# A two-layer attention trunk: compressed values and gate spread in row tiles, a sixth weight buffer, and a list schedule with pauses and an order table

## The chip, the cores and the metric

The kernel runs on one core of one Trainium2 chip. The core has a matrix engine (TensorE, PE in the profile; its weight loads are PEld), a vector engine (VectorE, DVE), a scalar engine (ScalarE, ACT), GpSimd (POOL) and a queue engine (SyncE, SP) that issues most loads. The metric is the device time of one execution in microseconds. All arithmetic is done in fp32 or in pairs of its rounded halves.

## The reference

`x` is 256 tokens of 1024 features. Each of two layers does `x = x + gate * mixer(h)`, where `shift, scale, gate` come from the vector `c` through `ada_w[i]` (1024 x 3072), and `h` is the RMS norm of `x`, scaled and shifted. Both mixers project `h`, attend with 16 query heads over 4 key heads of 64 features, multiply by `silu(z)` and project out:

```python
shift, scale, gate = split(silu(c) @ ada_w[i] + ada_b[i], 3)
h = rms_norm(x, norm_g[i]) * (1 + scale) + shift
# layer 1 (nsa): three attentions, each with its own gate per head
o = g0 * o_cmp + g1 * o_slc + g2 * o_win
# layer 2 (moba): with 256 tokens one block, so plain causal attention
x = x + gate * ((o * silu(z)) @ w_out)
```

In layer 1 `o_cmp` attends over 15 compressed keys and values: blocks of 32 tokens go through a small two-layer network per key head (`cmp_w1`, `cmp_w2`). `o_slc` and `o_win` come out, at this length, as two causal attentions with different keys and values.

## The kernel before

**Products.** An fp32 matrix is split into a rounded part `hi` and a rest `lo` (lines 624 to 631: ACT casts, DVE subtracts), and a product is three matmuls: hi by hi, hi by lo, lo by hi. A weight piece of 256 rows by 512 columns (512 KB) is loaded into one of five buffers `raw` (line 450) by SP; the last reader of `raw` is the subtraction into `lo`. PSUM has eight banks: two go by the name `acc`, for long accumulations, and six by the name `ps`, for everything else (lines 447, 448).

**Stages.** To about 58 us the first rows of `ada_w` and of the input projection are loaded into their own early buffers and multiplied as they land. Then come the rest of layer 1's projection with the compression network on its side, `make_q`, and eight pairs of heads (`pair_a(i)`, lines 1290 to 1331), with blocks of the `z` projection and layer 2's `ada_w` between them. The output projection (`out_products`) ends with the update of `x` and layer 2's norm (`next_h`, line 1348). Layer 2 does the same with `pair_b`, and its output projection ends in the stores.

**The two places in layer 1 that change.** The compressed attention of four pairs at once (`compressed(hf)`, line 1262) leaves `pcT[hf]`: 128 rows, which are 8 heads of 16 compressed keys, by 256 tokens. Pair `j_` needs only rows `32*j_` to `32*j_ + 31`. The kernel before multiplies all 128 rows by a matrix `Vbd[:, hf, j_]` that is zero outside those rows (lines 1239 to 1249 build it with the mask `emask`); the result starts the accumulation of the pair's output `o`, a `ps` bank, which `values` then adds to:

```python
o = tile_of("ps", 512)
T.matmul(o[:, 0:S], Vbd[:, hf, j_], pcT[hf], start=True, stop=False)
```

`values` (line 899) and the products by `condz` (line 640) use column tiles: parts of the matrix engine's columns, chosen by `tile_position`, so that several small products go on beside each other. The other place is `ada_gate(0)` (line 696): the gate of layer 1 arrives as row sums in `g`, and two full fp32 products with the 0/1 matrices `selG` add and spread them over all 128 partitions.

**Order.** Nothing is issued as the program runs. Each call records an operation with its dependencies, its buffers and a cost in ns (`record`, `_cost`), numbered in the order of the program. `Plan.issue` (line 231) then plays a list schedule: it keeps a clock for each engine, a clock for the DMA wire, and the times at which buffers come free; each step it takes, over all engines, the operation that can start first, ties going by level (urgent chain, chain, fill) and then by number. In that order the instructions are issued on each engine, loads into SP's queue included. The clocks of this planner decide only the order; on the chip each engine waits for semaphores. A product in column tiles that follows another one in tiles has a level of its own (`_rank`, line 223), and a change of the tiling adds 240 cycles of cost (line 335). All instructions carry the line of one helper, L373, so that they are told apart by the names of their tiles.

Of the kernel before, what the change touches and what calls it, by code (L numbers as in the profile page):

```python
# [9 lines left out]
F32 = mybir.dt.float32  # L10
# [4 lines left out]
OP = mybir.AluOpType  # L15
AX = mybir.AxisListType

P = 128
S = 256
# [3 lines left out]
HD = 64  # L23
# [11 lines left out]

TICK = 10240 / 3
DEEP = 2e4
TILED, LATER = -0.5, 0
SHORT_ROWS, SMALL, BEHIND, EARLY_RATE = 1.1, 7e4, 5500.0, 348.0
ISSUE, FIRST_BYTE, RATE, LANDED = 450.0, 1500.0, 315.0, 700.0  # L40


class Tag:
# [9 lines left out]
class Plan:  # L53
# [120 lines left out]
    def _cost(self, engine, method, args, kw, aps):  # L174
        def free(a):
            n = 1
            for _, k in a.ap[1:]:
                n *= k
            return n

        if "dma" in method:
            self.bytes = free(aps[0]) * aps[0].shape[0] * 4
            if aps[1].shape[-1] <= 128 and self.bytes > 1e5:
                self.bytes *= SHORT_ROWS
            if self.bytes <= 1e5:
                self.bytes += SMALL
            return max(ISSUE, self.bytes / RATE) if engine == "S" else ISSUE
        psum = any(str(a.space).endswith("PSUM") for a in aps)
        n = max(free(a) for a in aps)
        if engine == "T":  # L190
            if method == "transpose":
                return 262.0 if aps[1].dtype == F32 else 180.0
            cols = free(aps[2])
            if aps[2].dtype == F32:
                m = free(aps[1])
                if "tile_position" in kw and m <= 64:
                    return max(cols * 4.28 * max(32, m) / P, 60.0)
                return 2 * max(cols * 2.14, 264.0)
            return max(cols * (1.07 if aps[2].dtype == F32R else 1.0), 264.0)
        if engine == "A":  # L200
            return 0.833 * n + (51.0 if psum else 94.0) + 93.0 * sum(isinstance(kw.get(k), bass.AP) for k in ("bias", "scale", "accum_out"))
        if engine == "G":
            return 1.5 * n + 270.0
        if method == "reciprocal":
            return 6.5 * n + 68.0
        fast = not psum and (method == "tensor_copy" or method.startswith("tensor_scalar"))
        pointers = len(aps) - 2 if method.startswith("tensor_scalar") else 0
        return (0.521 if fast else 1.042) * n + 68.0 + 61.0 * pointers
# [22 lines left out]
    def issue(self, opening=()):  # L231
# [21 lines left out]
        for waiting, for_, call in opening:  # L253
            left = sum(len(self.tags[f].tiles) for f in for_)
            gate = {"left": left, "for": set(for_), "end": 0.0, "call": call, "called": False}
# [20 lines left out]
        tally, mode = {}, None  # L276
        ready = {e: [] for e in self.engines}
        for op in ops:
            op["at"] = 0.0
            if not op["wait"]:  # L280
                ready[op["engine"]].append(op)
        done = 0
        while done < len(ops):
            best = None
            for e, ops_e in ready.items():
                if not ops_e:
                    continue
                found = []
                first = None
                for op in ops_e:  # L290
                    t = max(clock[e], op["at"])
                    if first is not None and t > first and not (op["level"] < 0 and t <= first + self.AHEAD):
                        continue
                    blocked = False
                    for n in op["needs"]:
                        r = room(n)
                        if r is None:
                            blocked = True
                            break
                        t = max(t, r)  # L300
                    if blocked:
                        continue
                    found.append((t, self._rank(op, e, mode), op["id"], op))
                    first = t if first is None else min(first, t)
                pick = min(found, key=lambda f: f[:3]) if found else None
                if pick:
                    soon = [f for f in found if f[1] < 0 and f[1] < pick[1] and f[0] <= pick[0] + self.AHEAD
                            and f[0] < pick[0] + pick[3]["cost"]]
                    if soon:
                        pick = min(soon, key=lambda f: (f[1], f[0], f[2]))  # L310
                if pick and (best is None or pick[0] < best[0]):
                    best = pick + (e,)
            start, _, _, op, e = best
            ready[e].remove(op)
            for n in op["needs"]:
                t = self.tiles[n]
                if t["slot"] is None:
                    tag = t["tag"]
                    gate = closed.get(tag.name)
# [3 lines left out]
                    slot = min(tag.free)  # L323
# [8 lines left out]
            cost = op["cost"]  # L332
            if e == "T":
                tick = int(start // TICK)
                if op["mode"] != mode:
                    cost += 240.0
                mode = op["mode"]
                cost = cost * (1 / 2.4 if tally.get(tick - 1, 0.0) >= 3060.0 else 1 / 1.2)
                tally[tick] = tally.get(tick, 0.0) + op["cost"]
            end = start + cost  # L340
            clock[e] = end
            seen = end + self.SEEN[e]
# [10 lines left out]
            for n in op["needs"]:  # L353
                t = self.tiles[n]
# [11 lines left out]
            for a in after[op["id"]]:  # L366
                b = ops[a]
# [33 lines left out]
def kernel(  # L401
# [23 lines left out]
    nc = tc.nc  # L425
    ctx.enter_context(tc.manual_schedule())
    const = ctx.enter_context(tc.tile_pool(name="const", bufs=1))
    work = ctx.enter_context(tc.tile_pool(name="work", bufs=1))
    psum = ctx.enter_context(tc.tile_pool(name="psum", bufs=1, space=bass.MemoryType.PSUM))
    plan = Plan(nc)  # L430
    T, A, V, G, Q = plan.T, plan.A, plan.V, plan.G, plan.S
    tile_of = plan.tile
# [14 lines left out]
    plan.tag("acc", psum, 512, 2, space="PSUM")  # L447
    plan.tag("ps", psum, 512, 6, space="PSUM")
    plan.tag("early", early["pool"], 1024, 12)
    plan.tag("raw", work, 1024, 5)  # L450
    plan.tag("hi", work, 1024, 4, F32R)
    plan.tag("lo", work, 1024, 4, F32R)
    plan.tag("n_in", work, 1024, 2)
# [73 lines left out]
    nc.gpsimd.memset(maskC, 0.0)  # L527
    for m in range(2):
        keep(maskC[:, m, :], [[-16, 16]], m * P - 31)
    selG = const.tile([P, 2, P], F32, name="selG")  # L530
    nc.gpsimd.memset(selG, 0.0)
    nc.gpsimd.memset(selG[0:64, 0, :], 1.0)
    nc.gpsimd.memset(selG[64:128, 1, :], 1.0)
    ones = const.tile([P, P], F32, name="ones")
    nc.gpsimd.memset(ones, 1.0)
    identR = const.tile([P, P], F32R, name="identR")
    V.tensor_copy(identR, identF)
    emask = const.tile([P, 8], F32, name="emask")
    V.tensor_reduce(emask, identF.rearrange("p (j n) -> p j n", n=16), axis=AX.X, op=OP.add)


    RT = const.tile([P, ROWS], F32, name="RT")
# [153 lines left out]
    def ada_gate(l):  # L696

        gate = gates_of[l] = tile_of("gate", D)
        bias = bass.AP(tensor=ada_b.tensor, offset=ada_b.offset + l * 3 * D + 2 * D, ap=[[D, 1], [1, D]])
        if l:  # L700
            G.memset(gate, 0.0)
            Q.dma_start(gate[0:1], bias)
            for kk in range(8):
                w = ada_piece(l, kk, 2 * D, D)[:, 0, :]
                with plan.at(FILL):
                    V.scalar_tensor_tensor(gate, w, condz[:, kk, 0:1], gate, op0=OP.mult, op1=OP.add)
                yield
            mix, src = (ones, ones), (gate[:, 0:512], gate[:, 512:1024])
        else:
            g = yield from ada_rows(l, (2 * D, 2 * D + 512), 512)  # L710
            for s in range(2):
                Q.dma_start(g[64 * s + 1:64 * s + 2], bias[:, s * 512:(s + 1) * 512])
            mix, src = (selG[:, 0], selG[:, 1]), (g, g)
        for s in range(2):
            t = tile_of("ps", 512)
            with plan.at(FILL):
                T.matmul(t, mix[s], src[s], start=True, stop=True)
                A.copy(gate[:, s * 512:(s + 1) * 512], t)
# [350 lines left out]
    for k in range(2):  # L1069
# [16 lines left out]
        a, b = lead_w[k]  # L1086
# [149 lines left out]
                        kcs[:, 0, part].rearrange("p a d -> p (a d)"), identR[0:64, 0:64])  # L1236
    A.copy(KTA[:, :, :, 512:528], tk[:, 0:128].rearrange("p (a g n) -> p a g n", a=2, g=KVH))
    vb = tile_of("ps", 512)
    Vbd = const.tile([P, 2, 4, P], F32, name="Vbd")
    for hf in range(2):  # L1240
        for cc in range(2):
            uv = tile_of("pc", 2, 4, 16)
            V.tensor_copy(uv, u[:, cc, 1, 32 * hf:32 * hf + 32].rearrange("p (g n) -> p g n", g=2)[:, :, None, :]
                          .to_broadcast([P, 2, 4, 16]))
            T.matmul(vb[:, hf * HD:(hf + 1) * HD], uv.rearrange("p g r n -> p (g r n)"), w2[:, 1, cc, :],
                     start=(cc == 0), stop=(cc == 1))
        V.tensor_mul(Vbd[:, hf].rearrange("p j (e d) -> p (j e) d", e=2),
                     vb[:, None, hf * HD:(hf + 1) * HD].to_broadcast([P, 8, HD]),
                     emask[:, :, None].to_broadcast([P, 8, HD]))

    raw_q = tile_of("n_in", 2, 512)
    chunk(w_in, ((512, 512),), raw_part(raw_q, 512))
# [4 lines left out]
    z_later = z_blocks(w_in, 3120, zT)  # L1257


    pcT = {}  # L1260

    def compressed(hf):

# [26 lines left out]
    def pair_a(i):  # L1290
# [28 lines left out]
        for r in (1, 0):  # L1319
# [4 lines left out]
                return p1[r][:, e, 0, k * P:(k + 1) * P]  # L1324

            pT.insert(0, p_transposed(block))
        o = tile_of("ps", 512)
        T.matmul(o[:, 0:S], Vbd[:, hf, j_], pcT[hf], start=True, stop=False)
        vs = slice(g * HD, (g + 1) * HD)
        values(o, [([VA[:, m, 1 - r, vs] for m in range(2)], pT[r]) for r in (1, 0)], False)  # L1330
        gated(i, o, zT[i])
# [169 lines left out]
```

## Time and profile before

| | us |
|---|---|
| median of 3 runs | 317.1 (315.71 to 317.89) |
| profiled execution | 317.45 |
| its span | 315.7 |
| PE busy | 306.0 |
| PEld / DVE / ACT / POOL busy | 243.5 / 242.2 / 205.0 / 26.6 |
| DMA | 65.82 MB, mean 208 GB/s |

A row of a group names the line, the engine, the operation, `out<-in` by the names of the tiles, their shapes and the count; then the busy time, the mean length of one in ns, and the idle time in front. An fp32 product shows as two MATMUL instructions, a product of rounded halves as one. Matmuls overlap, so the distance between two starts, not the length, is what one costs. In the chain a row gives start, length and what the time went to.

### The profile page before, as it was taken

What the parts mean: (1) busy time and instruction counts of PE and PEld (TensorE: products, weight loads), DVE (VectorE), ACT (ScalarE), POOL (GpSimd) and SP (SyncE); (2) the same over time, 40 slices, a digit from 0 to 9 for tenths busy, and PEclk for the clock granted to TensorE, in tenths of its full rate; (3) what the DMA queues carried; (4) which work ended last, traced back from release to release, by engine and by line L of the source; (5) the groups of instructions that cost most, each with busy time, mean ns of one, the idle gap of its engine ahead of it and who ended that gap; (6) DMA issues with size and microseconds to landing.
All of it is one profiled execution on the core that took longest, in us unless ns stands there. A gap on an engine that the chain in (4) does not pass through costs nothing.

```text
span 315.7 us, 6158 instructions
## 1 busy us (share of the span) xinstructions
PE 306.0 (97%) x2133; PEld 243.5 (77%) x2133; DVE 242.2 (77%) x734; ACT 205.0 (65%) x486; POOL 26.6 (8%) x102
## 2 busy tenths in 40 slices
PE   4999999998999999999999999999999999999995
PEld 4666677777766797858879888877788999968784
DVE  4673374669982899835979887998599999999764
ACT  5735155764835787456799966786486489998420
POOL 8248900000000000000000000000000000000000
PEclk9999999999999999999999999999999999999999
DMA  7999999359899822788272377617188862423102
GB/s 248 320 357 367 368 359 323 111 171 311 279 309 306 277 79 90 246 304 250 113 261 76 116 217 226 240 60 212 65 261 263 298 229 84 155 69 120 59 34 102
DMA packets 44174, 65.82 MB, mean 208 GB/s; under 512 B 4221, under 2 KB 20971, under 8 KB 44142
## 3 DMA queue, kind: packets, MB, share of 16 engines
q1 hardware_dynamic: 43782, 65.36, 63.1%
q8 instruction: 17, 0.28, 0.4%
q14 instruction: 15, 0.12, 0.1%
q10 hardware_dynamic: 168, 0.06, 0.1%
q0 software_dynamic: 192, 0.00, 0.0%
HBM read 64.36 MB, written 1.05 MB: 207 GB/s over the span
## 4 chain that ended last, share of the span: by engine, by line
PE 90%; DMA 5%; ACT 2%; DVE 1%; issue 1%; SPq 0%; ACTq 0%; DVEq 0%
PE ps L373 54%; PE acc L373 36%; DMA raw<-in_nsa_w_in_dram 2%; DMA early<-in_ada_w_dram 2%; ACT hi L373 1%; DMA rot<-in_c_dram 0%; ACT n_in L373 0%; DVE lo L373 0%; DVE p L373 0%; ACT p L373 0%; DVE AB L373 0%; ACT HT L373 0%; DVE rot L373 0%; DVE y L373 0%; DVE X L373 0%
## 5 line engine op out<-in xcount | busy, mean ns | idle before, releaser
L373 ACT CAST hi<-raw 128x1024 fp32r<-128x1024 f32 (+1 forms) x48 | 48.8, 1023 | 25.5 <-DMA raw<-in_nsa_w_in_dram 9.8
L373 DVE TENSOR_TENSOR lo<-raw,hi 128x1024 fp32r<-128x1024 f32 (+1 forms) x48 | 56.4, 1181 | 11.0 <-ACT hi L373 10.8
L373 PE MATMUL acc<-hi,HT 128*128 128x512 f32 (+1 forms) x160 | 49.6, 381 | 1.3 <-ACT n_in L373 0.8
L373 ACT ACTIVATE p<-p,tiny 128x128 f32<-128x128 f32 (+1 forms) x96 | 43.2, 460 | 8.4 <-DVE tiny L373 8.3
L373 PE MATMUL acc<-HT,hi 128*128 128x256 f32 x192 | 37.8, 286 | 0.0
L373 PEld LDWEIGHTS acc<-hi,HT 128*128 128x128 f32 x160 | 29.1, 188 | 9.6 <-issue 2.9
L373 DVE CUSTOM_DVE_ANT_0 p<-ps,causal 128x128 f32<-128x128 f32 (+1 forms) x96 | 30.5, 346 | 3.1 <-PE ps L373 3.1
L373 PEld LDWEIGHTS acc<-HT,hi 128*128 128x128 f32 x192 | 30.1, 188 | 0.8 <-issue 0.7
L373 PE MATMUL acc<-lo,HT 128*128 128x512 f32 (+1 forms) x80 | 30.2, 380 | 0.2 <-DVE lo L373 0.2
L373 PE MATMUL ps<-hi,HT 128*128 128x512 f32 (+1 forms) x96 | 28.2, 365 | 0.0
L373 PE MATMUL acc<-HT,lo 128*128 128x256 f32 x96 | 27.8, 290 | 0.0
L373 PE MATMUL ps<-KTA,qg 128*128 128x256 f32 (+2 forms) x192 | 27.0, 284 | 0.0
L373 ACT COPY pT<-ps 128x384 f32<-128x384 f32 x48 | 21.5, 485 | 6.3 <-PE ps L373 6.2
L373 PEld LDWEIGHTS ps<-KTA,qg 128*128 128x128 f32 x192 | 24.2, 190 | 1.7 <-issue 1.2
L373 PE MATMUL ps<-hi,qg 128*128 128x256 f32 (+1 forms) x96 | 24.1, 323 | 0.0
L373 PE MATMUL acc<-hi,qg 128*128 128x512 f32 x64 | 22.8, 402 | 0.0
L373 PE MATMUL ps<-identF,p 128*128 128x128 f32 x144 | 21.7, 276 | 0.0
L373 PEld LDWEIGHTS ps<-hi,HT 128*128 128x128 f32 x96 | 17.0, 188 | 4.2 <-issue 2.1
L373 PEld LDWEIGHTS ps<-identF,p 128*128 128x128 f32 x144 | 16.4, 140 | 3.9 <-issue 1.2
L373 ACT ACTIVATION_READ_ACCUMULATOR p<-p,tiny 128x1 f32 x96 | 19.3, 201 | 0.0
L373 PE MATMUL ps<-pT,VA 128*64 128x256 f32 (+1 forms) x192 | 19.1, 334 | 0.0
L373 PEld LDWEIGHTS acc<-HT,lo 128*128 128x128 f32 x96 | 18.1, 189 | 0.1
(223 smaller groups left out, 614.5 us busy)
## 6 DMA issues: line engine op xcount, KB each, us to landing
raw<-in_ada_w_dram SPq DMA_DIRECT2D x32, 512.0 KB, 4.9
raw<-in_moba_w_in_dram SPq DMA_DIRECT2D x20, 512.0 KB, 4.3
early<-in_ada_w_dram SPq DMA_DIRECT2D x12, 512.0 KB, 9.5
raw<-in_nsa_w_in_dram SPq DMA_DIRECT2D x12, 512.0 KB, 6.4
early<-in_nsa_w_in_dram SPq DMA_DIRECT2D x9, 512.0 KB, 9.1
p<-in_nsa_cmp_w_dram SPq DMA_DIRECT2D x16, 256.0 KB, 3.8
raw<-in_nsa_w_out_dram SPq DMA_DIRECT2D x8, 512.0 KB, 5.7
raw<-in_moba_w_out_dram SPq DMA_DIRECT2D x8, 512.0 KB, 4.8
```

The costliest lines, as they stand in the source:

```text
L373: r = getattr(self.engines[e], method)(*[self._real(a) for a in args], **{k: self._real(a) for k, a in kw.items()})
```

## The change

- `pair_a`: at every even pair, two `ps` banks are taken, and one group holds two products in row tiles: rows `32*j` to `32*j + 31` of `Vbd` and `pcT`, at `tile_position=(32*j, 0)`, one bank each. The odd pair uses the second bank. `Vbd` has one block of 128 columns for each half where it had four, and `emask` two columns where it had eight.
- `ada_gate(0)`: one group of two products in row tiles of 64 rows, `ones` by the halves of `g`, into two banks; `selG` and its three fills are gone.
- `raw` has six buffers where it had five (the space of `Vbd` and `selG`).
- `_cost` prices row tiles, and the schedule lets an operation that needs several new buffers of one name wait until as many are free.
- The schedule adds `PAUSE` = 93 ns to a TensorE operation that crosses a boundary between ticks of 3413 ns. `LATER_BY` shifts the number by which ties are decided, for the operations named by their numbers; `HOLD` gives sixteen operations an earliest time in the planner's clock.

```diff
-TILED, LATER = -0.5, 0
+TILED, LATER, PAUSE = -0.5, 0, 93.0
...
+LATER_BY = [
+    (162, 162, -17), (329, 337, -24), (338, 338, 30), (344, 351, -111), (359, 366, -38), (372, 372, -38),
...
+    (1225, 1225, 22), (1240, 1245, -450), (1252, 1252, 90), (1291, 1296, 161), (1336, 1336, 45), (1342, 1348, 29),
...
+    (2413, 2413, -430), (2428, 2428, 923), (2469, 2470, 421),
+]
+SHIFT = {i: d for a, b, d in LATER_BY for i in range(a, b + 1)}
+HOLD = {
+    29: 2400, 32: 3700, 33: 3700, 51: 7200, 312: 35600, 391: 48800, 1276: 152700, 1340: 169100, 1350: 168000,
+    1415: 182100, 1573: 197400, 1576: 198800, 1579: 197400, 1585: 198700, 1636: 205200, 1655: 209300,
+}
...
-                m = free(aps[1])
-                if "tile_position" in kw and m <= 64:
-                    return max(cols * 4.28 * max(32, m) / P, 60.0)
+                m, rows = free(aps[1]), aps[1].shape[0]
+                if "tile_position" in kw and m * rows <= 64 * P:
+                    return max(cols * 4.28 * max(32, m) / P * max(32, rows) / P, 60.0) + (100.0 if rows < P else 0.0)
...
-            op["at"] = 0.0
+            op["at"], op["key"] = HOLD.get(op["id"], 0.0), op["id"] + SHIFT.get(op["id"], 0)
...
+                    new = {}
+                    for n in op["needs"]:
+                        if self.tiles[n]["slot"] is None:
+                            new.setdefault(self.tiles[n]["tag"].name, []).append(n)
+                    for name, several in new.items():
+                        if len(several) > 1 and not blocked:
+                            free = sorted(self.tags[name].free)
+                            blocked = len(free) < len(several)
+                            t = t if blocked else max(t, free[len(several) - 1][0])
...
-                    found.append((t, self._rank(op, e, mode), op["id"], op))
+                    found.append((t, self._rank(op, e, mode), op["key"], op))
...
+                if (start + cost) // TICK > tick:
+                    cost += PAUSE
...
-    plan.tag("raw", work, 1024, 5)
+    plan.tag("raw", work, 1024, 6)
...
-            mix, src = (selG[:, 0], selG[:, 1]), (g, g)
+            ts = [tile_of("ps", 512) for s in range(2)]
+            with plan.at(FILL):
+                with plan.group():
+                    for s in range(2):
+                        T.matmul(ts[s], ones[64 * s:64 * s + 64], g[64 * s:64 * s + 64], start=True, stop=True,
+                                 tile_position=(64 * s, 0))
+                for s in range(2):
+                    A.copy(gate[:, s * 512:(s + 1) * 512], ts[s])
+            return
...
-    Vbd = const.tile([P, 2, 4, P], F32, name="Vbd")
+    Vbd = const.tile([P, 2, P], F32, name="Vbd")
...
-        o = tile_of("ps", 512)
-        T.matmul(o[:, 0:S], Vbd[:, hf, j_], pcT[hf], start=True, stop=False)
+        if j_ % 2 == 0:
+            with plan.group():
+                for j in range(j_, j_ + 2):
+                    ov[hf, j] = tile_of("ps", 512)
+                    T.matmul(ov[hf, j][:, 0:S], Vbd[32 * j:32 * j + 32, hf], pcT[hf][32 * j:32 * j + 32],
+                             start=True, stop=False, tile_position=(32 * j, 0))
+        o = ov[hf, j_]
```

More of the change, by code (lines that the diff above doesn't have):

```diff
@@ L529 @@
         keep(maskC[:, m, :], [[-16, 16]], m * P - 31)
[L530 to L533, printed above, removed]
     ones = const.tile([P, P], F32, name="ones")
@@ L537 @@
     V.tensor_copy(identR, identF)
-    emask = const.tile([P, 8], F32, name="emask")
-    V.tensor_reduce(emask, identF.rearrange("p (j n) -> p j n", n=16), axis=AX.X, op=OP.add)
+    emask = const.tile([P, 2], F32, name="emask")
+    V.tensor_reduce(emask, identF.rearrange("p (j e n) -> p e j n", e=2, n=16), axis=AX.XY, op=OP.add)
     RT = const.tile([P, ROWS], F32, name="RT")
@@ L1246 @@
                      start=(cc == 0), stop=(cc == 1))
-        V.tensor_mul(Vbd[:, hf].rearrange("p j (e d) -> p (j e) d", e=2),
-                     vb[:, None, hf * HD:(hf + 1) * HD].to_broadcast([P, 8, HD]),
-                     emask[:, :, None].to_broadcast([P, 8, HD]))
+        V.tensor_mul(Vbd[:, hf].rearrange("p (e d) -> p e d", e=2),
+                     vb[:, None, hf * HD:(hf + 1) * HD].to_broadcast([P, 2, HD]),
+                     emask[:, :, None].to_broadcast([P, 2, HD]))
     raw_q = tile_of("n_in", 2, 512)
@@ L1257 @@
     z_later = z_blocks(w_in, 3120, zT)
-    pcT = {}
+    pcT, ov = {}, {}
     def compressed(hf):
```

9 rows, old and new, of the table LATER_BY are left out of this document.

## The prediction, made before the change was run

> **What bounds the kernel now.** I read the page first, for the engine shares and the chain that ended last.
>
> ```profile
> span 315.7 us, 6158 instructions
> ...
> PE 306.0 (97%) x2133; PEld 243.5 (77%) x2133; DVE 242.2 (77%) x734; ACT 205.0 (65%) x486; POOL 26.6 (8%) x102
> ...
> PE 90%; DMA 5%; ACT 2%; DVE 1%; issue 1%; SPq 0%; ACTq 0%; DVEq 0%
> ```
>
> TensorE (PE) is occupied for 306.0 of 315.7 us and is 90% of the chain, so every nanosecond taken out of its stream shortens the kernel, unless something that is late for another reason takes its place. The second view is the table by stages, to see where PE is not occupied (columns: stretch, its length, then busy time of PE, weight loads, DVE, ACT, POOL, granted clock, DMA share, GB/s).
>
> ```profile
> 0.00:10.00 10.00, 5.92 (x39) 4.81 (x39) 4.87 (x23) 5.13 (x8) 8.48 (x37) 1.00 0.82 265
> 10.00:20.00 10.00, 9.50 (x86) 6.36 (x86) 7.10 (x19) 7.05 (x13) 0.00 (x0) 1.00 1.09 336
> ...
> 30.00:40.00 10.00, 9.77 (x66) 6.48 (x66) 4.48 (x9) 3.46 (x5) 9.51 (x35) 1.00 1.08 364
> 60.00:70.00 10.00, 9.71 (x62) 6.76 (x61) 5.80 (x12) 8.38 (x22) 0.00 (x0) 1.00 0.43 130
> 70.00:80.00 10.00, 9.18 (x62) 7.97 (x61) 9.40 (x23) 4.99 (x8) 0.00 (x0) 1.00 0.94 314
> ...
> 160.00:170.00 10.00, 10.00 (x88) 8.81 (x88) 8.37 (x47) 9.97 (x36) 0.00 (x0) 1.00 0.61 209
> ...
> 200.00:210.00 10.00, 9.74 (x45) 7.18 (x44) 9.42 (x24) 8.53 (x21) 0.00 (x0) 1.00 0.29 95
> 310.00:316.00 6.00, 2.17 (x19) 1.96 (x17) 2.45 (x6) 0.00 (x0) 0.00 (x0) 1.00 0.25 88
> ```
>
> The granted clock is 1.00 in all of them, so the clock is no part of the argument. Of the 9.7 us that PE is idle, 4.08 lie in the first stretch and about 3.6 behind the last product (5.74 less 2.17). Between them the five shown stretches lose 0.50, 0.23, 0.29, 0.82 and 0.26: 2.10 us. PE busy hides more, since its matmuls overlap: a wait shorter than a matmul's tail shows only as a larger distance between starts. Two places show what ends such waits. The first, in the chain (start, length, what), in SP's waits from 55 to 80 us (in all, times, longest), and in PE's timeline:
>
> ```profile
> 69.66 0.37 SPq L373
> ...
> 70.08 6.94 DMA raw<-in_nsa_w_in_dram
> ...
> 77.12 1.05 ACT hi L373
> 78.17 0.28 ACT n_in L373
> ```
>
> ```profile
> SPq L373 <- DVE lo L373: 10.8, 3, 4.1
> ```
>
> ```profile
> 77.38 0.30 PE L373 MATMUL acc<-hi,HT 128*128 128x304 f32 x1
> 78.49 0.50 PE L373 MATMUL acc<-hi,HT 128*128 128x512 f32 x1 [0.82 <-ACT n_in L373]
> ...
> 202.42 0.39 PE L373 MATMUL ps<-hi,qg 128*128 128x512 f32 x1
> 202.65 0.39 PE L373 MATMUL ps<-lo,qg 128*128 128x512 f32 x1
> ...
> 204.97 0.40 PE L373 MATMUL ps<-lo,qg 128*128 128x512 f32 x1
> 205.53 0.44 PE L373 MATMUL ps<-identF,n_in 128*128 128x128 f32 x2 [0.16 <-ACT n_in L373]
> 205.72 0.47 PE L373 MATMUL ps<-hi,qg 128*128 128x512 f32 x1
> 206.29 0.33 PE L373 MATMUL ps<-identF,n_in 128*128 128x128 f32 x1
> ```
>
> At 78 us the last copy out of an accumulator (`n_in`) stands on ACT behind a cast of a weight piece, and that cast stands behind a load issued at 69.66; SP had waited 10.8 us in this stretch for `DVE lo`, the last reader of a `raw` buffer. The second place is 205 us: PE's starts are 0.56 and 0.57 us apart behind products of a form that follow each other at 0.23 (202.42, 202.65): the next layer's `n_in` scaling is late on ACT.
>
> **The change, part by part.** The profiled execution took 317.45 us: its span of 315.7 and 1.75 around it, 0.35 above the median 317.1. The sum is made from 317.45.
>
> *Compressed values.* Eight full fp32 products (`pcT`, `Vbd`) become four groups of two row tiles of 32 rows.
>
> ```profile
> L373 PE MATMUL ps<-pcT,Vbd x16: 377/379/483, 135.1 to 171.3; 128*128 128x256 f32 x16
> L373 DVE TENSOR_TENSOR Vbd<-ps,emask x2: 673/675/677, 115.6 to 118.0; 128x512 f32<-128x512 f32 x2
> ...
> 161.86 1.03 PE L373 MATMUL ps<-pcT,Vbd 128*128 128x256 f32 x4
> ...
> 135.06 0.62 PE L373 MATMUL ps<-pcT,Vbd 128*128 128x256 f32 x2
> 135.62 1.52 PE L373 MATMUL ps<-pT,VA 128*64 128x256 f32 x16
> 137.07 0.64 PE L373 MATMUL ps<-raw,condz 128*32 128x512 f32 x4
> ```
>
> Sixteen instructions for eight products: two passes each. Four in a row take 1.03 us of which the last one's 0.379 is its own length, so a pass costs (1.03 - 0.38)/3 = 0.217 and a product 0.43 us; eight cost 3.46. No row-tiled pair is in this trace. The nearest row is the column-tiled `pT,VA`: its 16 passes, half of 256 columns and half of 128, would take 8 x 0.217 + 8 x 0.109 = 2.6 us one after the other, but the next work starts 1.45 us after them, so two tiles run beside each other. I take the same for row tiles: a pair costs one product, 4 x 0.43 = 1.73. Each pair is a visit to another tiling and back, and that has a price in these rows:
>
> ```profile
> 100.87 0.28 PE L373 MATMUL acc<-HT,lo 128*128 128x256 f32 x1
> 100.98 0.28 PE L373 MATMUL acc<-HT,hi 128*128 128x256 f32 x1
> 101.19 0.98 PE L373 MATMUL ps<-p,p 128*64 128x256 f32 x4
> ...
> 18.26 0.99 PE L373 MATMUL ps<-y,ones 1*128 1x432 f32 x2
> 19.17 0.51 PE L373 MATMUL ps<-hi,HT 128*128 128x512 f32 x1
> ```
>
> A product start is 0.11 after the last, and 0.21 when the tiling changes: 0.10 a change. The one-row product takes 0.91 us for two passes of 432 columns, where 2 x 0.217 x 432/256 = 0.73 would do: 0.18, again about 0.09 each way. Four visits: 4 x 0.18 = 0.72. So -3.46 + 1.73 + 0.72 = **-1.0 us**. Ends: -1.73 if every pair falls inside another tiled stretch and pays no change, +0.7 if the two tiles do not overlap. That `Vbd` has a quarter of its columns takes about 3/4 of 2 x 0.675 off DVE; PE is not waiting for it there, so it counts nothing.
>
> The Trainium skill, "TensorE: Matmul & The Clock Gate", Part 3 (Measured speedup vs the span model), gives four row tiles 3.07 times the speed of one after the other, not four; by an estimate from that page a pair costs 1.3 x 0.43, and this term would be -0.5 instead of -1.0.
>
> *The gate.* Four passes of 512 columns become two tiles of 64 rows.
>
> ```profile
> 119.48 1.88 PE L373 MATMUL ps<-row,selG 128*128 128x512 f32 x4
> ...
> 121.19 0.27 PE L373 MATMUL ps<-identF,p 128*128 128x128 f32 x1
> ```
>
> From 119.48 to 121.19 is 1.71; half of it and two changes is 0.86 + 0.18, so **-0.7** (-0.85 inside a tiled stretch, +0.2 without overlap). Its two copies by ACT stay. The three POOL fills of `selG` go; PE waits for none of them.
>
> *The sixth `raw` buffer.* The load at 69.66 could be issued as soon as SP reaches it, up to the 4.1 us that SP's longest wait lasted. The cast at 77.12 would follow earlier, and the 0.82 us hole goes: **-0.8**. Next late is the ACT copy itself. Low end -1.1 (starts at 77.38 and 78.49 less one product); high end +1.4: a further 512 KB at the 364 GB/s of the stretch 30:40 put ahead of a load that is needed sooner.
>
> *The pauses, the holds and the order table.* They change no instruction, only the order on each engine and in SP's queue; the pause makes the planner's clock slower. The entries name, by operation number, ACT's and DVE's steps of the next layer's norm (around 205 us), score, softmax and transpose steps of the pairs (100 to 180 and 250 to 290 us), loads of both layers, and a few first loads. Against this stands what can be had: the idle of the middle without the hole at 78 us is 2.10 - 0.82 = 1.28, which I count as gone, since the numbered steps stand at those places; and visits to the tiled form that can be joined.
>
> ```profile
> L373 PE MATMUL ps<-pT,VA 128*64 128x256 f32 (+1 forms) x192 | 19.1, 334 | 0.0
> ```
>
> 192 passes are 16 visits (eight pairs of layer one by 16, eight of layer two by 8), each 0.18 us in and out: 2.9 us. If a quarter disappear by standing beside another tiled stretch, that is 0.7. So **-2.0**; low end -1.28 - 1.45 (half of the visits) = -2.7, high end nothing won and waits newly made, up to the size of those that are there now, +2.1.
>
> Sum: -1.0 - 0.7 - 0.8 - 2.0 = -4.5, so 317.45 - 4.5 = 312.95 for a profiled execution, and **312.6** for the median.
>
> **The rivals.**
>
> *No gain worth the name.* Row tiles run one after the other (+0.7 + 0.2), the sixth buffer's load is late for another reason (0), and the table moves work about between waits of equal size (0 to -1.3). That gives 317.1 + 0.9 - 0.0 to 1.3 = 316.7 to 318.0. For it: the trace holds no row-tiled group at all, and PE is shown at 10.00 of 10 us in the pair stage, so a merely different order of the same products ends at the same time. Against it: the column tiles overlap.
>
> *Slower, by the banks of `ps`.* The even pair now takes two `ps` banks, and the second is held until the odd pair's values are done. From the `Vbd` row, eight pairs span 135.1 to 171.3, 5.2 us each; four such holds leave five of six banks for 4 x 5.2 = 21 us. A pair passes eight tiles through these banks (three scores, four transposes, one output). If their turn sets the pace, 21 us become 21 x 6/5: +4.2 us, and what PE saves on `Vbd` there is hidden. With the gate's -0.7 and nothing else that is 317.1 + 4.2 - 0.7 = 320.6, slower by 1.1%. It decides when ACT and DVE empty banks later than PE has other work to do. For it: ACT is busy 9.97 of 10 us at 160 to 170 us, and weight loads already wait for ACT's results:
>
> ```profile
> PEld ps L373 <- ACT p L373: 2.2, 4, 0.8
> ...
> PEld ps L373 <- ACT pT L373: 1.1, 3, 0.4
> ```
>
> Against it: those waits do not reach PE (10.00 there), because the products into `acc` fill in. The Trainium skill, "TensorEngine Tiling (Array Packing)", Gotcha 1: PSUM Pressure, says that row tiles write to different banks and raise the pressure on them; by that page this rival is the one to fear, and no run here shows it yet.
>
> **How the numbers follow.** About 1% is what a measurement of this kernel can tell from no change: faster means below 313.9, slower above 320.3. The forecast has a chance of 0.65, no gain 0.23, the banks 0.12. The forecast's own spread (its terms' ends give 317.1 - 6.4 = 310.7 and, with the order's gain lost, 314.6) puts about 0.55 below 313.9 and 0.10 above it. So faster 0.55, same 0.10 + 0.23 = 0.33, slower 0.12. The range takes the forecast from its low end, with 0.7 us more for the first loads in the 4.08 idle us of the start, to the no-gain case's 318.0: 310.0 to 318.0. Outside lie the bank rival and some 0.06 below.
>
> **What would show it.** The `pcT,Vbd` passes with 32 rows: the two tiles' starts a few ns apart, 0.43 us until the next work, not 0.87. The gate's tiles: about 0.9 us instead of 1.71. PE's stretch 70:80 near 9.9 or more, and no load ahead of the cast in the chain there. The stretch 200:210 near 10. The stretches between 130 and 180 still at 10.00: if they fall, with PE waiting for ACT `p`, `pT` or DVE `p`, the banks decide. I am wrong if PE's busy time falls by about 2 us and the time does not, or if the idle of the middle grows past 2.1.

## The result

| | median us | runs |
|---|---|---|
| before | 317.36 | 315.71 to 317.89 (4) |
| changed | 312.77 | 312.48 to 313.15 (4) |

The ratio is 0.9878, with a 95% interval of 0.9855 to 0.99: faster by 1.2%. The profiled execution of the changed kernel took 312.48 us, 310.7 of it the span, against 317.45 and 315.7. In a later set of runs the changed kernel took 313.42 against 316.91: 0.9899 (0.9866 to 0.9933). Three of the twelve executions of one kernel below, the order without its table, ran some 4 us longer at a granted clock of 0.99; its time is given without them.

The page of the changed kernel, shares and chain:

```profile
span 310.7 us, 6167 instructions
...
PE 301.6 (97%) x2133; PEld 242.0 (78%) x2133; DVE 242.0 (78%) x734; ACT 205.1 (66%) x486; POOL 28.2 (9%) x99
...
PE 90%; DVE 3%; DMA 3%; ACT 2%; issue 1%; ACTq 0%; SPq 0%; DVEq 0%
```

PE has as many instructions as before and bounds the kernel as before; it is 4.4 us less busy. Its stretches, in the same columns as in the prediction:

```profile
0.00:10.00 10.00, 5.87 (x35) 5.15 (x39) 5.71 (x25) 5.12 (x8) 7.35 (x34) 1.00 0.87 264
10.00:20.00 10.00, 9.86 (x97) 6.70 (x88) 6.17 (x17) 6.71 (x13) 0.00 (x0) 1.00 1.11 340
...
30.00:40.00 10.00, 9.87 (x67) 6.76 (x66) 5.32 (x8) 4.12 (x6) 9.43 (x28) 1.00 1.08 363
...
60.00:70.00 10.00, 9.49 (x62) 6.69 (x61) 5.44 (x11) 8.44 (x22) 0.00 (x0) 1.00 0.58 167
70.00:80.00 10.00, 10.00 (x65) 8.35 (x65) 9.17 (x22) 5.83 (x8) 0.00 (x0) 1.00 0.95 313
...
150.00:160.00 10.00, 9.99 (x88) 9.20 (x88) 10.00 (x50) 9.72 (x32) 0.00 (x0) 1.00 0.67 210
160.00:170.00 10.00, 10.00 (x84) 8.48 (x83) 10.00 (x30) 9.69 (x27) 0.00 (x0) 1.00 0.39 121
...
200.00:210.00 10.00, 9.74 (x50) 7.73 (x48) 9.27 (x23) 8.96 (x23) 0.00 (x0) 1.00 0.26 68
210.00:220.00 10.00, 9.97 (x46) 7.61 (x45) 5.39 (x10) 4.96 (x14) 0.00 (x0) 1.00 0.54 162
...
240.00:250.00 10.00, 9.74 (x90) 9.54 (x88) 10.00 (x18) 5.95 (x9) 0.00 (x0) 1.00 0.80 263
```

The idle of the start is as it was (4.13, 4.08 before). That of the middle is 0.14 + 0.13 + 0.51 + 0.01 + 0.26 + 0.03 + 0.26 = 1.34 us, where it was 2.10. The hole at 78 us is closed (9.18 to 10.00), the wait of the next layer's norm is not (9.74 in both), and the stretch 60:70 is worse by 0.22. The pair stage shows 9.99 and 10.00. A second profiled execution of the same kernel (the run `after_again`) has a part of the hole left, 0.25 us:

```profile
77.14 0.51 PE L404 MATMUL acc<-hi,HT 128*128 128x512 f32 x1 [0.25 <-DVE tiny L404]
```

The row tiles, in the tile's summary and in PE's timeline:

```profile
L404 PE MATMUL ps<-pcT,Vbd x16: 374/426/479, 136.3 to 160.7; 32*128 32x256 f32 x16
```

```profile
108.97 1.13 PE L404 MATMUL ps<-row,ones 64*128 64x512 f32 x4
110.03 0.44 PE L404 MATMUL ps<-identF,g 128*128 128x128 f32 x2
...
136.28 0.70 PE L404 MATMUL ps<-pcT,Vbd 32*128 32x256 f32 x4
136.91 0.76 PE L404 MATMUL ps<-pT,VA 128*64 128x256 f32 x6
...
142.66 0.70 PE L404 MATMUL ps<-pcT,Vbd 32*128 32x256 f32 x4
143.29 0.55 PE L404 MATMUL ps<-identF,p 128*128 128x128 f32 x3
...
160.19 0.28 PE L404 MATMUL acc<-HT,hi 128*128 128x256 f32 x1
160.39 0.71 PE L404 MATMUL ps<-pcT,Vbd 32*128 32x256 f32 x8
161.04 0.39 PE L404 MATMUL acc<-HT,hi 128*128 128x256 f32 x1
```

A pair of row tiles (4 passes) takes 0.63 us until the next work, and the last two groups, which the order put beside each other, take 0.65 for all four products (8 passes). One after the other two products would take 0.87 and four 1.73 us. So the tiles do run at the same time. The gate takes 1.06 us instead of 1.71.

A second count is needed below: how often PE changes its tiling. Going through the matmuls in order of their starts, a change is counted wherever the form becomes another one of these: full, column tiles of 64, column tiles of 32, or row tiles, all but the first by `tile_position`. There are 79 changes before and 67 in the changed kernel. Counted only as full or in column tiles, they are 70 and 54; the forecast of the split run below uses these two.

### The profile page after: what moved, and what is told of

It is laid out like the page before. It is cut to its first block, busy times and chain, and to the rows that moved or that the text cites. A ratio compares the mean times of both kernels' runs of the same rounds, so it can differ in the third digit from the quotient of the medians.

```text
span 310.7 us, 6167 instructions
## 1 busy us (share of the span) xinstructions
PE 301.6 (97%) x2133; PEld 242.0 (78%) x2133; DVE 242.0 (78%) x734; ACT 205.1 (66%) x486; POOL 28.2 (9%) x99
## 4 chain that ended last, share of the span: by engine, by line
PE 90%; DVE 3%; DMA 3%; ACT 2%; issue 1%; ACTq 0%; SPq 0%; DVEq 0%
PE ps L404 52%; PE acc L404 38%; DMA y<-in_ada_b_dram 2%; DMA early<-in_nsa_w_in_dram 1%; ACT hi L404 1%; DVE lo L404 1%; DVE rs L404 1%; DVE y L404 0%; ACT n_parts L404 0%; ACTq L404 0%; DVE X L404 0%; DVE p L404 0%; ACT n_out L404 0%; ACT HT L404 0%; DVE n_parts L404 0%
## 5 line engine op out<-in xcount | busy, mean ns | idle before, releaser
L404 ACT CAST hi<-early 128x1024 fp32r<-128x1024 f32 (+2 forms) x17 | 14.9, 896 | 13.1 <-DMA early<-in_nsa_w_in_dram 8.9
L404 PE MATMUL ps<-hi,qg 128*128 128x256 f32 (+1 forms) x96 | 23.4, 326 | 0.0
L404 DVE TENSOR_TENSOR lo<-early,hi 128x1024 fp32r<-128x1024 f32 (+2 forms) x17 | 17.6, 1047 | 5.9 <-ACT hi L404 5.9
L404 PE MATMUL acc<-hi,qg 128*128 128x512 f32 x64 | 21.7, 405 | 0.0
```

The lines of the kernel that those rows point to most:

```text
L404: r = getattr(self.engines[e], method)(*[self._real(a) for a in args], **{k: self._real(a) for k, a in kw.items()})
```

## The experiments

All are timed in five rounds against the kernel before on the same chip; the three sets ran on three chips, so between sets the ratios are the surer measure. The first set asks whether the tiles, the buffer and the order each act by their own cost; the changed kernel itself ran beside them.

> The changed kernel once more, as the common measure for the runs beside it. Both theories: 312.8 us, 0.986 of the kernel before.

It took 313.42 us, ratio 0.9899 (0.9866 to 0.9933): 0.6 us above what was expected. The differences in this set are taken from 313.42.

**The tiles undone at their places.** The order is kept; only the operands are those of full products.

```diff
             T.matmul(ov[hf, j][:, 0:S], Vbd[32 * j:32 * j + 32, hf], pcT[hf][32 * j:32 * j + 32], ...)
+        plan.ops[-1]["calls"] = [(m_, (x_[0], Vbd[:, hf], pcT[hf]), dict(start=True, stop=False))
+                                 for m_, x_, _ in plan.ops[-1]["calls"]]
...
+        plan.ops[-1]["calls"] = [(m_, (x_[0], ones, g), dict(start=True, stop=True))
+                                 for m_, x_, _ in plan.ops[-1]["calls"]]
```

> The changed kernel with every instruction at its place, but the row tiles replaced by products over all 128 rows (two passes of 0.217 us each for the compressed values, of 0.43 for the gate), as the kernel before had them in size. What is left out: the products are not limited to their rows, so the compressed values of a pair and the gate hold sums over other rows too. Theory 1 (each part acts by its own cost on TensorE): by the trace of the changed kernel two groups of 0.63 us become 0.87, the joined pair of groups 0.645 becomes 1.73, the gate's 1.06 becomes 1.71, less some 0.4 for changes of tiling: +1.8 us, 314.6 us, ratio 0.991. Theory 2 (the order carries the gain, what the tiles save is taken up by waits elsewhere): at most +0.4 us, 313.2, ratio 0.987.

It took 315.06 us, ratio 0.9941 (0.992 to 0.9962): 1.6 us above the changed kernel beside it. In its timeline the eight passes that took 0.65 us start 0.215 us apart, which is 1.72 in all:

```profile
161.95 1.89 PE L404 MATMUL ps<-pcT,Vbd 128*128 128x256 f32 x8
163.49 0.47 PE L404 MATMUL acc<-HT,hi 128*128 128x256 f32 x1
163.79 0.28 PE L404 MATMUL acc<-HT,lo 128*128 128x256 f32 x1
```

(The start of the next product, at 163.49, is shown 0.03 us after the eighth pass's own start; the one behind it follows 0.31 later.) Theory 1 said 1.8, theory 2 at most 0.4. In this order the tiles' saving on PE is a saving of the whole.

**Five buffers under the table.**

```diff
-    plan.tag("raw", work, 1024, 6)
+    plan.tag("raw", work, 1024, 5)
```

> The changed kernel with five raw buffers in place of six, table and holds kept; the planner puts loads later. Theory 1: the wait at 78 us comes back, +0.8 us, 313.6, ratio 0.988. Theory 2 (the order was made for six buffers and carries the gain): it falls apart, +2 us or more, 314.8 or more, ratio 0.992 or more. If the buffer does nothing: 312.8.

It took 324.19 us, ratio 1.0221 (1.018 to 1.0262): 10.8 us above the changed kernel. That is theory 2, far beyond the 2 us that it named as the least. The place of the sixth buffer's forecast shows a part of it:

```profile
77.68 0.30 PE L404 MATMUL acc<-hi,HT 128*128 128x304 f32 x1
79.54 0.50 PE L404 MATMUL acc<-hi,HT 128*128 128x512 f32 x1 [1.56 <-DVE tiny L404]
```

PE idles 1.56 us there, behind the reading of the accumulator that `DVE tiny` does. From 10 us on it idles 6.1 us in all, where the changed kernel has 1.3.

**The order without its table.**

```diff
-LATER_BY = [ (162, 162, -17), ... ]
+LATER_BY = []
-HOLD = { 29: 2400, ... }
+HOLD = {}
```

> The changed kernel with the order table and the holds empty, pauses kept. Theory 1: the order was worth some 2 us in the sum, of which the pauses keep a part: +1.5 us, 314.3, ratio 0.990. Theory 2: the order carries nearly all of 4.6 us: 316.5 or more, ratio 0.997 or more. If the table does nothing: 312.8.

It took 316.05 us, ratio 0.9975 (0.9955 to 0.9996). Against the changed kernel that is 2.6 us, between theory 1's 1.5 and the 3.7 of theory 2, whose ratio it reaches: the table and the holds are worth more than the 2 us that the forecast gave to the order with the pauses, and not all of the gain. Changes of tiling: 83, where the changed kernel has 67. The second set builds the change up from the other side, and halves the table.

```diff
 # tiles_alone: row tiles; no table, no holds, and
-TILED, LATER, PAUSE = -0.5, 0, 93.0
+TILED, LATER, PAUSE = -0.5, 0, 0.0
-    plan.tag("raw", work, 1024, 6)
+    plan.tag("raw", work, 1024, 5)
 # tiles_six_raw: the same with 6
 # no_hold: the changed kernel with HOLD = {};  no_shift: with LATER_BY = []
```

> The row tiles alone: five raw buffers, no pauses, no table, no holds. Theory 1 (each part acts by its own cost): the changed trace gives about 1.4 us less for the compressed values and 0.6 for the gate: 317.4 - 2.0 = 315.4, ratio 0.994. Theory 2 (the order carries the gain): 317.0 to 317.8, ratio 0.999 to 1.001. The bank rival of the prediction: slower, 319 or more.

It took 315.98 us, ratio 0.9973 (0.9953 to 0.9992): 0.85 us less than before, where theory 1 expected 2.0 and theory 2 nothing. The tiles do their work at the same time here too, but the order made with them has 85 changes of tiling, 6 more than before. It is not slower, as the rival of the banks would have it.

> Row tiles and six raw buffers; no pauses, no table, no holds. Theory 1: 0.8 us less than the row tiles alone: 314.6, ratio 0.991. Theory 2: as the row tiles alone, 317.0 to 317.8.

It took 314.60 us, ratio 0.993 (0.9909 to 0.9952): 1.4 us less than the tiles alone, where theory 1 expected 0.8. But the gain is not at 78 us. The stretch and PE's timeline, with five buffers:

```profile
70.00:80.00 10.00, 9.53 (x63) 8.33 (x63) 9.43 (x25) 5.24 (x9) 0.00 (x0) 1.00 0.97 322
```

```profile
77.47 0.30 PE L388 MATMUL acc<-hi,HT 128*128 128x304 f32 x1
78.24 0.50 PE L388 MATMUL acc<-hi,HT 128*128 128x512 f32 x1 [0.47 <-ACT n_in L388]
```

and with six, where ACT's timeline shows the copy at 76.65, ahead of the cast and of any late load:

```profile
70.00:80.00 10.00, 9.55 (x64) 7.99 (x65) 9.47 (x22) 6.06 (x11) 0.00 (x0) 1.00 0.95 320
```

```profile
77.02 0.30 PE L388 MATMUL acc<-hi,HT 128*128 128x304 f32 x1
77.77 0.50 PE L388 MATMUL acc<-hi,HT 128*128 128x512 f32 x1 [0.45 <-DVE tiny L388]
```

```profile
76.65 0.36 ACT L388 COPY n_in<-acc 128x256 f32<-128x256 f32 x1
77.36 0.37 ACT L388 COPY n_in<-acc 128x256 f32<-128x256 f32 x1 [0.35 <-PE acc L388]
77.63 1.05 ACT L388 CAST hi<-raw 128x1024 fp32r<-128x1024 f32 x1
```

The load is no longer late and PE waits as long as before: 0.45 us instead of 0.47, now for `DVE tiny`, the other reader of the accumulator.

> The changed kernel without the sixteen holds; the shifts kept. Theory 1: part of the order's 2 us is lost, +0.5 to +1.5 us, 313.3 to 314.3. Theory 2 (table and holds were found together, one is nothing without the other): as far as no table at all or worse, 315 to 317.

> The changed kernel without the shifts; the sixteen holds kept. Theory 1: part of the order's 2 us is lost, +0.5 to +1.5 us, 313.3 to 314.3. Theory 2 (table and holds were found together, one is nothing without the other): as far as no table at all or worse, 315 to 317.

Without the holds it took 316.23 us, ratio 0.9984 (0.9957 to 1.001); without the shifts 316.51, ratio 0.9985 (0.9965 to 1.0005). Neither half does better than no table at all (0.9975); theory 2 of these two runs holds. Neither half has a worth of its own here; single entries were not tried.

The third set asks what the table does, and what the pauses do.

```diff
 # split_visits, in values(): between the first and the second half of the group
+        calls.insert(len(calls) // 2, ("matmul", (o[:, 300:316], identF, identF[:, 0:16]), ...))
 # plain_control, in p_transposed(): at the end of the second group
+                plan.ops[-1]["calls"].append(("matmul", (t[:, 400:416], identF, identF[:, 0:16]), ...))
 # five_raw_no_table: LATER_BY = [], HOLD = {}, five buffers, pauses kept
 # before_pause: the kernel before, and in the schedule
+                if (start + cost) // TICK > tick:
+                    cost += PAUSE
```

> The changed kernel in its own order; in the middle of each of the sixteen groups of pair values (column tiles) stands one more small full product of 16 columns, into unused columns of the bank. It adds sixteen returns from the tiled form and sixteen entries. Theory A (the table's gain is mostly visits to the tiled form that it joined: the starts show 70 changes of tiling before and without the table, 54 in the changed kernel): 0.18 us a visit over the control run beside it, +2.9 us, about 0.9 to 1.0% more than the control. Theory B (changes of tiling are hidden, the table's gain is elsewhere): the same time as the control.

> The same sixteen small products, each at the end of a group of full transposes, so that no change of tiling is added. Both theories: sixteen times the small product itself, 0.03 to 0.11 us each (two passes of 16 columns): +0.5 to +1.8 us over the changed kernel's 312.8.

The split kernel took 318.80 us, ratio 1.0066 (1.0048 to 1.0085); the control 315.33, ratio 0.9948 (0.9932 to 0.9963). The difference is 3.47 us for sixteen visits, 0.22 us each, or 0.11 a change (32 more: 99 against 67). (The control itself is 1.9 us above the 313.42 of the first set, or 1.6 by the ratios; 0.5 to 1.8 was expected.) One of them in the timeline of the split kernel, and the same group in the control:

```profile
138.25 0.87 PE L404 MATMUL ps<-pT,VA 128*64 128x256 f32 x8
139.05 0.40 PE L404 MATMUL ps<-identF 128*128 128x16 f32 x2
139.37 0.87 PE L404 MATMUL ps<-pT,VA 128*64 128x256 f32 x8
```

```profile
137.93 1.52 PE L404 MATMUL ps<-pT,VA 128*64 128x256 f32 x16
139.38 1.06 PE L404 MATMUL ps<-raw,condz 128*32 128x512 f32 x8
```

From the first half's start to the second's are 1.12 us, where half of the control's group takes 0.73 (1.45/2): 0.39 for the small product and two changes. Changes of tiling are not hidden: that half of theory A holds. Its other half, that the table gains mostly by them, is an estimate: with 83 changes without the table and 67 with it, at this price the joined visits give 16 x 0.11 = 1.7 of the 2.6 us. That is not the whole: the run without the holds has 75 changes and is no faster than the one without any table, with more idle time on PE (below).

> Row tiles, five raw buffers, pauses; no table, no holds. Theory A (the loss of 7 us with five buffers under the table is a table out of step with its plan): near the run without table and with six buffers, 315.5 to 317.5, ratio 0.995 to 1.001. Theory B (the sixth buffer itself is worth that much once pauses are counted): 320 or more, ratio 1.009 or more.

> The kernel before with the pauses counted in the planner and nothing else. Theory A (the pauses by themselves make the order no better; row tiles and six buffers gave 0.993 without and 0.9975 with them): 317 to 319, ratio 1.000 to 1.005. Theory B (they bring the plan nearer to the chip and help; the loss seen was chance of one order): 315 to 316.5, ratio 0.993 to 0.998.

Five buffers without the table took 319.68 us, ratio 1.0101 (1.0079 to 1.0123); the kernel before with the pauses 320.41, ratio 1.0124 (1.0092 to 1.0156). For five buffers the ratio is that of theory B, and the time 0.3 us short of it. So the loss under the table is three steps, none of them small. By the ratios (0.9899, 0.9975, 1.0101, 1.0221) they are 2.4 us without the table, 4.0 more without the sixth buffer as well, and 3.8 more when the table is laid over the plan with five buffers, for which it was not made. With the pauses counted and nothing else the kernel before is slower by 1.2%, more than either theory said. PE's idle time from 10 us on grows by 1.5 us. The longest new wait is in layer 2, where the kernel before had no idle time on PE (50.0 of 50 us from 250 to 300):

```profile
250.00:260.00 10.00, 8.84 (x79) 8.65 (x79) 10.00 (x21) 5.45 (x7) 0.00 (x0) 1.00 0.87 295
```

```profile
258.21 0.28 PE L375 MATMUL acc<-HT,lo 128*128 128x256 f32 x1
259.64 0.53 PE L375 MATMUL ps<-identR,n_parts 128*128 128x128 f32 x4 [1.16 <-DVE n_parts L375]
```

PE waits 1.16 us for the splitting of the queries, which is one of the things that DVE, busy 10.00 of 10 us, does in this stretch. The rest of the loss is not traced.

All runs in one table. "Idle" is PE's idle time between 10 us and its last product, from the stretches of the profile; "changes" the changes of tiling. (The profiled execution of the split kernel is its longest, 320.18 us; 0.8 of its idle time is one wait for a load at 81 us, ahead of the pairs.)

| kernel | us | ratio | idle | changes |
|---|---|---|---|---|
| before | 316.87 to 317.36 | 1 | 2.1 | 79 |
| tiles alone | 315.98 | 0.9973 | 1.8 | 85 |
| tiles, six buffers | 314.60 | 0.9930 | 2.7 | 81 |
| tiles, six buffers, pauses | 316.05 | 0.9975 | 2.2 | 83 |
| and the shifts, no holds | 316.23 | 0.9984 | 3.1 | 75 |
| and the holds, no shifts | 316.51 | 0.9985 | 2.7 | 79 |
| changed (all of it) | 312.77, 313.42 | 0.9878, 0.9899 | 1.3 | 67 |
| changed, full products | 315.06 | 0.9941 | 1.6 | 62 |
| changed, five buffers | 324.19 | 1.0221 | 6.1 | 77 |
| tiles, five buffers, pauses | 319.68 | 1.0101 | 3.5 | 85 |
| before, pauses | 320.41 | 1.0124 | 3.6 | 78 |
| changed, visits split | 318.80 | 1.0066 | 2.0 | 99 |
| changed, control of it | 315.33 | 0.9948 | 1.6 | 67 |

## Why the prediction was right, and where it was not

The time was right: 312.6 forecast, 312.77 measured, and 313.42 in the later set. The rows are of the profiled executions, which are 5.0 us apart (317.45 and 312.48), and they account for most of it. The passes of the tiles fell from 3.46 + 1.71 to 0.63 + 0.63 + 0.65 + 1.06, which is 2.2 us (some of it the changes at their ends, so the sum is rough); 12 changes of tiling fewer at 0.11 are 1.3; the middle's idle is 0.76 less: 4.3 of the 5.0 us. But two terms were wrong in size and two in their cause. That they made up for each other to 0.2 us was luck.

**Compressed values, -1.0.** The step that they overlap is shown: 0.63 us for a pair, not 0.87 or more. Mis-sized was the visit. Its two passes at 0.217 would be 0.43, but it takes 0.63, and where it is entered out of full products another 0.09 (the starts at 136.07 and 136.28 are 0.21 apart, where 0.11 would do). The way in and out is 0.3 us, not 0.18. I had read the 0.18 off the one-row product from its own start on and left its entry out, which is 0.09 as well (18.05 to 18.26). On the other side there were three visits, not four, since two groups stand together. In all 3.46 became 1.91 us and some 0.2 for entries out of full products, -1.4.

Is the 0.2 us inside the visit a dearer pass in row tiles, or the change of tiling? Each of the two passes takes 0.31 to 0.32 us, but one is the first of its visit and the other the last. Other forms pay at these places too. In the column tiles `p,p` and `pT,VA` a pass of 256 columns takes 0.216 us in the middle of a visit and 0.27 as the first, and in `p,p` 0.32 as the last before another form. And in the run with full products, the first pass of the gate behind column tiles takes 0.53, the other three 0.43 each, 1.82 in all:

```profile
109.39 1.98 PE L404 MATMUL ps<-row,ones 128*128 128x512 f32 x4
111.21 0.38 PE L404 MATMUL ps<-identF,g 128*128 128x128 f32 x2
```

This speaks for the change, but it is not shown: no run has a pass that is clearly in the middle of a visit to row tiles. (In the run with five buffers and no table two groups follow each other, and the passes between them also take 0.31; but the second group's weight load waits there for ACT `pT`.)

The Trainium skill's "TensorE: Matmul & The Clock Gate", Part 3 (Measured speedup vs the span model), gives four row tiles 3.07 times the speed. Here four at once took 0.65 us against 1.73, 2.7 times, with the entry not counted.

**The gate, -0.7.** Measured -0.56: 1.06 us and 0.09 for the entry instead of 1.71, again because the way in and out is 0.3 us (0.53 a pass instead of 0.43, and the entry) and not 0.18. Both together were tested by the full products: 1.6 us on the whole.

**The sixth buffer, -0.8.** The hole closed, but the step named for it fails. With the tiles alone, a sixth buffer brings the load in time, and PE waits 0.45 us there all the same, for DVE's reading of the accumulator. I had named the ACT copy as what is late next, and missed that the accumulator has a second reader. What closes the hole in the changed kernel is not settled. The shifts go with it: without them 0.24 us of a wait for `DVE tiny` is left there, without the holds none. Yet the second execution of the changed kernel has such a wait too, 0.25 us. The buffer's 1.4 us in that pair of runs are elsewhere (where, the runs do not show), and its worth depends on the order: 1.4 us without pauses, 4.0 with them, 10.8 under a table made for six.

**Pauses, holds and table, -2.0.** From the row-tiled kernel with six buffers (0.993) to the whole change (0.9878 and 0.9899) the order gave 1.0 to 1.6 us. The prediction took this as one step; it is two of opposite sign. The orders made with the pauses were worse: by 0.45% with six buffers (0.993 to 0.9975), by 1.2 to 1.3% with five. Table and holds then gave 2.4 to 3.1 us. The mechanism of joined visits was right, and sized too small: I counted a quarter of 16 visits at 0.18, 0.7 us; it was 16 changes fewer than without the table, 1.7 us at the measured price. That all of the middle's other idle time, 1.28 us, would go since the entries stand at those places was wrong: it is 1.34 us now, and 0.26 of it is at 200:210 as before. That an entry stands at a place did not mean that it shortens the wait there.

**The rivals.** No gain: the tiles overlap, so its ground fell; yet tiles alone, at 0.9973, came near it. That the new order gave back part of what they saved (6 changes more, 0.7 us by the price above) is likely and was not tested. The banks: with two `ps` banks taken for each pair of pairs, PE is busy 9.99 and 10.00 of 10 in the pair stage at 150 to 170 us, and the tiles alone were not slower. ACT and DVE are full there, as the prediction feared, and PE has other work. By the Trainium skill's "TensorEngine Tiling (Array Packing)", Gotcha 1 (PSUM Pressure), the pressure on the banks rises. No run here shows a cost that can be put down to it.

**The first loads.** The 0.7 us that the low end took from them did not come: 4.13 us idle in the first stretch, 4.08 before.

## What to carry to other kernels

On an engine that is busy to the last, a product's price is its distance to the next start, and a change of tiling has one too (0.11 us here for column tiles, some 0.15 for row tiles): count both, in the order as it is issued, not as written. A table of order corrections is worth what it is worth only with the plan, the buffers and the costs it was made for; with one buffer less it cost some 4 us here where it had given 2.4 to 3.1. Test a part of such a change with the order kept, instruction by instruction, or the order's own swing, one to four microseconds here, can hide what the part does.

## What the runs showed that was not expected

A visit to row tiles costs about 0.3 us beyond its passes, so two row tiles beside each other save little at 256 columns (0.63 us and 0.09 for the entry, against 0.87), while four at once save over half (0.65 and 0.09, against 1.73). And a planner's cost that is meant to bring its clock nearer to the chip made the kernel before slower by 1.2% on its own (320.41 against 316.87 us). It changes nothing but the order, so this order was the worse one; that it came nearer to the chip was not tested.
